# A two-layer mixer and MLP step on one core: side work looked for at every row tile, LRU factors computed inside ScalarE's functions

## The chip, the cores and the metric

The kernel runs on one core of one Trainium2 chip. Its five engines are TensorE (PE in the profile; its weight loads are shown apart as PEld), VectorE (DVE), ScalarE (ACT), GpSimd (POOL) and SyncE (SP), which here only issues transfers. The metric is the device time of one launch in microseconds, lower being better; it is given as the median of several runs.

## The reference, cut to what matters

One inference step of a backbone with two layers. 128 context tokens and 256 latent tokens (384 in all, width 1024, float32) go through each layer; the two groups share the weights but have modulation vectors of their own. Each layer is a mixer of four parallel branches and an MLP, each with a norm before and one behind it:

```python
def trunk_layer(x, cond, P, l, ctx):
    sh1, sc1, g1, sh2, sc2, g2 = modulation(cond, P['ada_w'], P['ada_b'])   # silu(cond) @ (1024 x 6144)
    h = rmsnorm(x, P['norm_mix_pre']) * (1.0 + sc1) + sh1
    y, ctx_out = mixer(h, P, l, ctx)
    x = x + g1 * rmsnorm(y, P['norm_mix_post'])
    h = rmsnorm(x, P['norm_ffn_pre']) * (1.0 + sc2) + sh2
    y = jnp.square(jax.nn.relu(h @ P['mlp_w1'])) @ P['mlp_w2']
    return x + g2 * rmsnorm(y, P['norm_ffn_post']), ctx_out
```

The mixer multiplies h by w_in (13 column groups) and computes A, neighbourhood attention (with a bias table of its own); B, differential attention; C, retention in both directions; D, the RG-LRU in both directions. Two parts of it are touched here:

```python
# retention, one direction: decay inside a chunk of 128 tokens
dmat = jnp.where(mask, jnp.exp(jnp.where(mask, rel, 0.0) * lg[:, None, None]), 0.0)
inner = jnp.einsum('bhnd,bhmd->bhnm', qc, kc) * dmat
# RG-LRU, one direction
r = sigmoid(block_diagonal(x, wa) + ba);  i = sigmoid(block_diagonal(x, wx) + bx)
log_a = -LRU_C * r * softplus(-lam)
a = exp(log_a);  u = sqrt(-expm1(2.0 * log_a)) * (i * x)      # then a linear scan over the tokens
yd = hd * gelu(lr_g)
# the branches are merged
y = (sum over branches of sigmoid(gate_k) * (y_k @ w_branch_k)) @ w_out
```

## The kernel before, in words

**The long products.** All weight products are computed from two-part splits: a weight block is loaded as float32 (tile `raw`) and split into a high part `wh` (ScalarE, sometimes VectorE) and a low part `wl` (VectorE), and the activations likewise (`hh`, `hl` for h; `yh`, `yl` for a branch's result). Each product is three products: high by high, high by low, low by high. `triple` (line 898) issues these three for each row tile k of the contraction, into a PSUM tile `mm`, and yields behind every second k. These products form one stream in a fixed order. For a layer's mixer, in counts of single products: up to 696 the groups of branches B and D, 696 to 792 branch B's gate columns, then its merge; 984 to 1176 retention's q and k; 1176 to 1272 branch D's gates; from 1272 its merge with `w_branch`; 1464 to 1728 the groups of branch A; 1728 branch C's gates; 2016 branch A's gates; 2304 to 2448 `w_out`. A whole layer with its MLP has 3540.

**The side work.** Everything else of the mixer (attention scores, retention, LRU gates, transposes, and the modulation of the next norms, tagged `ada`) is written as generators. `later` (line 611) puts one into a queue with the tag of the branch whose result it belongs to (`yA` to `yD`, or `ada`). `poll` (line 634) runs wherever the stream yields: it goes through the active generators and advances those whose needed tiles are ready by the planner's clock, unless VectorE or ScalarE is more than `BACKLOG = 2.25` us ahead of TensorE. `drain_side` (line 650) runs what is left of a tag, ready or not, where the stream comes to that branch's merge (`need_y`, line 1600).

**The planner.** All this happens while the program is built. `Clock` (line 55) keeps a modelled time for each engine; `Engine` (line 137) wraps every engine, works out a cost for each operation in `cost` (line 165), and books it in `note` (line 101). Hence nearly every operation is recorded at one line, L149. So the costs only set the order in which each engine's instructions are written; on the chip each engine works through its own list and waits for its semaphores. In `note` a VectorE operation that reads SBUF is charged 22% more for the time in which GpSimd is booked as busy. The one-column powers (`small<-small,mhalf 128x1`, a reciprocal square root for a norm) cost 0.52 in `cost`.

**Branch D's side work.** `lg_evac` (line 1217) evacuates the gate input of the RG-LRU, queues the `gelu` of a row tile under `yB`, and `lru_tile` (line 1243) under `yD`: block-diagonal gate products (`y<-setB_x,bia`), tanh on ScalarE, a scaling on VectorE (`tmp<-tmp,lp 128x386`, 16 times), exp and tanh, then the scan, and the split into `yh` and `yl`. Its tile of 386 columns holds 384 tokens and two starts.

**Branch C's side work.** `ret_pair` (line 1356) makes a pair of retention's heads: first the decay tiles (128 x 384 for each head: a `tensor_scalar` and a `scalar_tensor_tensor` over all columns on VectorE, the smaller of two multiples, then exp on ScalarE), then scores, products with v (`y<-v,big`), a norm of the result (`small`, a power on GpSimd, `tmp<-y,small`) and transposes by TensorE (`y<-ident,tmp`). Four pairs in each layer.

**The modulation steps** (`ada`, line 812) take a block of `ada_w`, loaded by SyncE into tile `half`, and add it, times the condition, into an accumulator on VectorE: `big<-half,condT,big 128x512`.

**Branch A's bias** is loaded by GpSimd's queue (`bia<-in_na_rpb`) and given its mask on GpSimd (`bia<-bia,cst`).

Of the kernel before, what the change touches and what calls it, by code (L numbers as in the profile page):

```python
# [55 lines left out]
class Clock:  # L56
# [3 lines left out]

    def __init__(self):
        self.eng = dict(PE=0.0, ACT=0.0, DVE=0.0, POOL=0.0, SP=0.0, Q=0.0, DMA=0.0)
        self.read = {}
        self.ready, self.used, self.slots, self.by, self.free_at, self.parts = {}, {}, {}, {}, {}, {}

    def alloc(self, t, tag, bufs):
# [34 lines left out]
    def note(self, eng, cost, outs, ins, dma=0.0):  # L101
        s = self.eng[eng]
        if eng == "DVE" and any(a.space != PSUM for a in ins):
            cost += 0.22 * max(0.0, min(cost, self.eng["POOL"] - s))
        for a in ins:
            s = max(s, self.when(a, eng))
            if a.space == PSUM:

                by, t = self.read.get(a.name, (eng, 0.0))
                if by != eng:  # L110
                    s = max(s, t + self.HOP[by])
        for a in outs:
            s = max(s, self.free_at.get(a.name, 0.0))
        e = s + cost
        self.eng[eng] = e
        if dma:
            q = self.eng["Q"] = max(self.eng["Q"], e) + 0.47
            e = self.eng["DMA"] = max(self.eng["DMA"], q + 1.6) + dma
            e += 0.9
        for a in ins:  # L120
            if a.space == PSUM:
                self.read[a.name] = (eng, e)
            self.used[a.name] = max(self.used.get(a.name, 0.0), e)
        for a in outs:
            for k in self.keys(a):
                self.ready[k] = e
                self.by[k] = "SP" if dma else eng
            self.used[a.name] = max(self.used.get(a.name, 0.0), e)
# [9 lines left out]
class Engine:  # L138
# [26 lines left out]
    def cost(self, name, aps, k, a):  # L165
        if name == "dma_start":
            return dict(SP=0.06, ACT=0.55, POOL=0.63)[self.key]
        n = max(_size(x) for x in aps)
        psum = any(x.space == PSUM for x in aps)
        if self.key == "ACT":  # L170

            table = (AF.Sqrt in a) if a[2:] and a[2] not in (AF.Copy, AF.Square, AF.Identity, AF.Relu) else self.table
            load = 1.29 if self.table is not None and table != self.table else 0.0
            self.table = table
            half = 0.12 if aps[0].shape[0] == 64 else 0.0
            return load + half + (0.05 if psum else 0.094) + n / 1200 + 0.09 * (len(aps) - 2)
        if self.key == "POOL":
            if k.get("op") == ALU.pow:
                return 0.3 + 0.22 * n
            return 0.1 + n / (290 if name == "tensor_copy" else 390)  # L180
        if self.key == "PE":
            n = _size(aps[0])

            cut = tuple(next(x for x in (32, 64, 128) if a.shape[0] <= x) for a in (aps[1], aps[0]))
            if name == "transpose":
                cut = (128, 128)
            place = (aps[1].start_partition(), aps[0].start_partition())
            switch = 0.0 if cut == self.cut else 0.1
            t = 0.107 if name == "transpose" else max(n / 2195, 0.107) if aps[1].dtype == F32R else max(n / 612, 0.22)
            if switch or cut == (128, 128) or place in self.places:  # L190
                self.places = []
            beside = bool(self.places)
            self.cut = cut
            self.places.append(place)
            return switch + (0.014 if beside else t)
        if name == "reciprocal":
            return 0.07 + n / 120
        if name == "tensor_tensor_scan":
            return 0.04 + n / 425
        extra = 0.06 * sum(x.shape[-1] == 1 for x in aps[1:])  # L200
        if name in ("tensor_scalar", "tensor_copy") and not psum:
            return 0.07 + n / 1920 + extra
        return 0.07 + n / 960 + extra
# [17 lines left out]
def hybrid_flow_kernel(ctx: ExitStack, tc: tile.TileContext, I, O):  # L221
# [272 lines left out]

    RUSH = (0.3, 0.0, 0.0)
    BACKLOG = 2.25

    ADA_LOADS = 3
    ADA_BACKLOG = 1.0
# [133 lines left out]

    def poll():
        admit()
        for task in sorted(active, key=lambda t: t["tag"] == "ada"):
            now = clock.eng["PE"]
            if max(clock.eng["DVE"], clock.eng["ACT"]) > now + BACKLOG or clock.free("y", 6, 2) > now or state["held"] > 4:
                return

            if task["tag"] == "ada" and clock.eng["DVE"] > now + ADA_BACKLOG:
                continue
            need = task["need"]
            n = getattr(need, "n", 0)
            if state["held"] + n > 6 or clock.free("y", 6, max(n, 1)) > now:
                continue
            if need() if callable(need) else clock.at(need) <= now:
                advance(task)
# [249 lines left out]
    def triple(p, pairs):  # L898
        n = len(pairs)
        for i, (ah, al, bh, bl) in enumerate(pairs):  # L900
            mm(p, ah, bh, start=i == 0, stop=False)
            mm(p, ah, bl, start=False, stop=False)
            mm(p, al, bh, start=False, stop=i == n - 1)
            if i % 2:
                yield

    def add_proj_cm(l, c0, n, H, evac, pre=None):

# [58 lines left out]
    def add_layer(l):  # L967
# [212 lines left out]


        S["xd"], S["gg"], S["yD"] = [None] * 4, [None] * 4, [None] * 4
        NL = 386

        def atile():
# [19 lines left out]
                    yield  # L1205
            S["xd"][j] = xd

        def gelu(a, gv):
            yield (a,)
            dve.tensor_scalar(a, a, 0.044715, 1.0, op0=ALU.mult, op1=ALU.add)  # L1210
            dve.tensor_mul(a, a, gv)
# [1 line left out]
            act(a, a, AF.Tanh, scale=GELU_C)  # L1213
            yield (a,)
            dve.scalar_tensor_tensor(gv, a, 1.0, gv, op0=ALU.add, op1=ALU.mult)

        def lg_evac(j, p):
            g = ctile("setB_g")
# [2 lines left out]
            a = atile()[:, 0:NTOK]  # L1221
            act(a, p, AF.Square)
            S["gg"][j] = g
            later(gelu(a, gv), "yB")
            later(lru_tile(j), "yD", (7, 0))
            if j == 3:
                later(S["split_yD"](), "yD")
# [13 lines left out]
                    SP.dma_start(dst, I[n][l, 4 * jh:4 * jh + 4].rearrange("(j q) d e -> (q d) j e", q=2))  # L1241

        def lru_tile(j):
            while "kl" not in LP[l] or S["xd"][j] is None:
                yield
            xd = S["xd"][j][:, 0:NL]
            yield (xd, *S["bia"])
# [20 lines left out]
            for d in range(2):  # L1268
# [1 line left out]
                kl = P("kl")[:, d, j:j + 1]  # L1270
                L, u = ths
                yield (L, u)
                dve.tensor_scalar(L, L, kl, kl, op0=ALU.mult, op1=ALU.add)
                dve.scalar_tensor_tensor(u, u, 1.0, xd, op0=ALU.add, op1=ALU.mult)
                a = tmp()[:, 0:NL]
                act(a, L, AF.Exp)
                act(L, L, AF.Tanh)
                sq = tmp()[:, 0:NL]
                act(sq, a, AF.Square)
                yield (sq,)  # L1280
# [75 lines left out]
        def ret_pair(j):  # L1356
# [3 lines left out]
            for hh in range(2):  # L1360
                h = 2 * j + hh
                a = tmp()[:, 0:384]
                rel = cst[:, C_REL:C_REL + 384]
                dve.tensor_scalar(a, rel, P("nlb")[:, h:h + 1], None, op0=ALU.mult)
                dve.scalar_tensor_tensor(a, rel, P("lg")[:, 0, h:h + 1], a, op0=ALU.mult, op1=ALU.min)
                act(a, a, AF.Exp)
                Dm.append(a)
                yield
            qx = []
# [626 lines left out]
```

## Time and profile before

| | us |
|---|---|
| median of 3 runs (1659.6, 1664.07, 1659.7) | 1659.7 |
| the profiled execution | 1663.42 |
| its span | 1661.6 |
| TensorE busy | 1617.7 |
| VectorE busy | 1172.9 |
| ScalarE busy | 720.0 |
| GpSimd busy | 225.8 |

The span is the time from the first to the last instruction of the profiled execution; what lies outside it is start and end, 1.8 us. "Busy" is the time in which an engine has an instruction under way. In a row of a timeline a value in brackets is the idle time of the engine just ahead of the row, and behind the arrow stands what released it. The granted clock is the share of TensorE's full 2.4 GHz that it was given in a stretch.

### The profile page before, as it was taken

How to read it: one execution, taken by the hardware profiler on the slowest of the kernel's cores; microseconds unless marked ns; L12 is line 12 of the kernel's file. 1: busy time of each engine (PE TensorE's matmuls, PEld its weight loads, DVE VectorE, ACT ScalarE, POOL GpSimd, SP SyncE). 2: the span in 40 equal slices, each digit the busy share in tenths (PEclk: the TensorE clock that was granted, in tenths of full speed). 3: DMA queues.
4: the chain of work that ended last, by engine and by line, in shares of the span. 5: the costliest groups of instructions: out<-in, count | busy, mean ns of one | idle time of the engine just before them, and what ended most of it. 6: DMA issues, size and time to landing. Idle time of an engine off the chain costs nothing.

```text
span 1661.6 us, 24134 instructions
## 1 busy us (share of the span) xinstructions
PE 1617.7 (97%) x9274; PEld 1477.6 (89%) x9274; DVE 1172.9 (71%) x2065; ACT 720.0 (43%) x1389; POOL 225.8 (14%) x290
## 2 busy tenths in 40 slices
PE   6999999999999999999999999999999999999998
PEld 4999998988899898888899999998988988888897
DVE  3696778888796647777678766788878766484444
ACT  3245666333442733333452547633344246333333
POOL 3310100342310100000021110023322100000000
PEclk8999999999999999999999999999999999999999
DMA  9433334357544335656453233445763362463332
GB/s 347 152 117 102 102 121 171 130 143 189 158 150 167 126 106 204 223 196 209 135 164 125 85 115 120 141 156 170 175 166 119 136 215 70 142 215 132 130 125 89
DMA packets 181829, 250.80 MB, mean 151 GB/s; under 512 B 22481, under 2 KB 126722, under 8 KB 181714
## 3 DMA queue, kind: packets, MB, share of 16 engines
q1 hardware_dynamic: 167938, 240.61, 42.9%
q0 software_dynamic: 3936, 5.94, 2.9%
q10 hardware_dynamic: 9840, 2.71, 0.7%
q8 instruction: 73, 1.20, 0.3%
q14 instruction: 42, 0.34, 0.1%
HBM read 243.40 MB, written 5.81 MB: 150 GB/s over the span
## 4 chain that ended last, share of the span: by engine, by line
PE 66%; DVE 7%; ACT 2%; DMA 2%; issue 1%; DVEq 0%; POOLq 0%; SPq 0%; ACTq 0%
PE mm L149 39%; PE y L149 28%; DVE wl L149 2%; DVE tmp L149 2%; DVE big L149 1%; DMA raw<-in_w_in 1%; ACT tmp L149 1%; DMA half<-in_ada_w 1%; ACT big L149 1%; DVE small L149 1%; ACT wh L149 0%; DVE wh L149 0%; ACT half L149 0%; DVE acc L149 0%; DVE half L149 0%
## 5 line engine op out<-in xcount | busy, mean ns | idle before, releaser
L149 PE MATMUL mm<-hh,wh 128*128 128x384 f32 x1536 | 528.1, 344 | 3.6 <-DVE acc L149 2.1
L149 DVE TENSOR_TENSOR wl<-raw,wh 128x1024 fp32r<-128x1024 f32 x315 | 396.2, 1259 | 178.7 <-ACT wh L149 171.2
L149 PE MATMUL mm<-hh,wl 128*128 128x384 f32 x1536 | 518.6, 338 | 0.0
L149 PE MATMUL mm<-hl,wh 128*128 128x384 f32 x1536 | 518.5, 338 | 0.0
L149 ACT ACTIVATE wh<-raw 128x1024 fp32r<-128x1024 f32 x252 | 265.0, 1055 | 215.6 <-PE y L149 131.9
L149 PEld LDWEIGHTS mm<-hh,wh 128*128 128x128 f32 x1536 | 289.0, 188 | 20.4 <-issue 10.4
L149 PEld LDWEIGHTS mm<-hl,wh 128*128 128x128 f32 x1536 | 289.3, 188 | 1.3
L149 PEld LDWEIGHTS mm<-hh,wl 128*128 128x128 f32 x1536 | 288.9, 188 | 0.0
L149 DVE SCALAR_TENSOR_TENSOR big<-half,condT,big 128x512 f32<-128x512 f32 x224 | 168.9, 791 | 5.0 <-DMA half<-in_ada_w 5.0
L149 PE MATMUL y<-wh,yh 128*128 128x512 f32 x312 | 123.4, 396 | 0.0
L149 PE MATMUL y<-wh,yl 128*128 128x512 f32 x312 | 123.3, 395 | 0.0
L149 PE MATMUL y<-wl,yh 128*128 128x512 f32 x312 | 123.2, 395 | 0.0
L149 PE MATMUL mm<-yh,wh 128*128 128x384 f32 x256 | 90.3, 353 | 6.4 <-ACT yh L149 2.9
L149 POOL TENSOR_TENSOR small<-small,mhalf 128x1 f32<-128x1 f32 (+2 forms) x40 | 37.0, 926 | 434.0 <-DVE small L149 434.0
L149 ACT ACTIVATE tmp<-mm 128x384 f32<-128x384 f32 x64 | 31.5, 492 | 143.6 <-PE mm L149 143.6
L149 DVE CAST wh<-raw 128x1024 fp32r<-128x1024 f32 x64 | 44.3, 692 | 63.0 <-PE mm L149 55.3
L149 PE MATMUL mm<-yl,wh 128*128 128x384 f32 x256 | 87.3, 341 | 0.1
L149 PE MATMUL mm<-yh,wl 128*128 128x384 f32 x256 | 87.2, 341 | 0.0
L149 PE MATMUL y<-wh,hh 128*128 128x512 f32 (+1 forms) x192 | 75.1, 391 | 0.2 <-DVE hh L149 0.2
L149 PE MATMUL y<-wh,hl 128*128 128x512 f32 (+1 forms) x192 | 73.8, 384 | 0.3 <-DVE hl L149 0.3
L149 PE MATMUL y<-wl,hh 128*128 128x512 f32 (+1 forms) x192 | 73.7, 384 | 0.0
L149 PEld LDWEIGHTS y<-wl,yh 128*128 128x128 f32 x312 | 58.5, 187 | 14.2
(333 smaller groups left out, 2457.9 us busy)
## 6 DMA issues: line engine op xcount, KB each, us to landing
raw<-in_w_in SPq DMA_DIRECT2D x80, 1024.0 KB
raw<-in_mlp_w SPq DMA_DIRECT2D x64, 1024.0 KB
half<-in_ada_w SPq DMA_DIRECT2D x160, 256.0 KB
raw<-in_w_branch SPq DMA_DIRECT2D x16, 1024.0 KB
raw<-in_w_out SPq DMA_DIRECT2D x8, 1024.0 KB
v<-gscr SPq DMA_DIRECT2D x16, 256.0 KB
bia<-in_na_rpb POOLq DMA_DIRECT2D x32, 96.0 KB, 8.4
raw<-in_ada_w SPq DMA_DIRECT2D x4, 512.0 KB
```

The lines of the kernel that those rows point to most:

```text
L149: r = f(*a, **k)
```

## The change

Five edits. (1) `triple` yields behind every k, so that `poll` runs behind every 3 products of such a piece instead of every 6. (2) `poll` goes through the active generators in the order yB, yD, yC, yA, ada, instead of the order in which they were queued with ada last. (3) The gelu of branch D has the tag yD, and an LRU tile waits (in the planning) until its gelu has been made. (4) The scaling of the LRU is taken into ScalarE's exp and tanh, as a scale and a bias for each partition; the decay tiles are made in three column blocks, since left and right of the diagonal block only one of the two multiples counts: VectorE does the middle 128 columns, ScalarE's exp has the factor as its scale in the outer ones and runs three times. (5) In the planner, a one-column power costs 0.46, and VectorE is charged beside GpSimd only for GpSimd operations of more than 64 elements.

```diff
@@ note
-            cost += 0.22 * max(0.0, min(cost, self.eng["POOL"] - s))
+            cost += 0.22 * max(0.0, min(cost, self.wide - s))
@@ 
+        if eng == "POOL" and _size(outs[0]) > 64:
+            self.wide = e
@@ cost
-                return 0.3 + 0.22 * n
+                return 0.46 if n == 1 else 0.3 + 0.22 * n
@@ poll
+    DUE = ("yB", "yD", "yC", "yA", "ada")
...
-        for task in sorted(active, key=lambda t: t["tag"] == "ada"):
+        for task in sorted(active, key=lambda t: DUE.index(t["tag"]) if t["tag"] in DUE else 0):
@@ triple
-            if i % 2:
-                yield
+            yield
@@ gelu, lg_evac, lru_tile
+            S["gelu"].add(j)
...
-            later(gelu(a, gv), "yB")
+            later(gelu(a, gv, j), "yD")
             later(lru_tile(j), "yD", (7, 0))
...
-            while "kl" not in LP[l] or S["xd"][j] is None:
+            while "kl" not in LP[l] or S["xd"][j] is None or j not in S["gelu"]:
                 yield
...
-                dve.tensor_scalar(L, L, kl, kl, op0=ALU.mult, op1=ALU.add)
+                a = tmp()[:, 0:NL]
+                act(a, L, AF.Exp, scale=kl, bias=kl)
+                act(L, L, AF.Tanh, scale=kl, bias=kl)
                 dve.scalar_tensor_tensor(u, u, 1.0, xd, op0=ALU.add, op1=ALU.mult)
-                a = tmp()[:, 0:NL]
-                act(a, L, AF.Exp)
-                act(L, L, AF.Tanh)
@@ ret_pair
-                dve.tensor_scalar(a, rel, P("nlb")[:, h:h + 1], None, op0=ALU.mult)
-                dve.scalar_tensor_tensor(a, rel, P("lg")[:, 0, h:h + 1], a, op0=ALU.mult, op1=ALU.min)
-                act(a, a, AF.Exp)
+                l_, m_, r_ = slice(0, 128), slice(128, 256), slice(256, 384)
+                lf, lb = P("lg")[:, 0, h:h + 1], P("nlb")[:, h:h + 1]
+                dve.tensor_scalar(a[:, m_], rel[:, m_], lb, None, op0=ALU.mult)
+                dve.scalar_tensor_tensor(a[:, m_], rel[:, m_], lf, a[:, m_], op0=ALU.mult, op1=ALU.min)
+                act(a[:, l_], rel[:, l_], AF.Exp, scale=lb)
+                act(a[:, r_], rel[:, r_], AF.Exp, scale=lf)
+                act(a[:, m_], a[:, m_], AF.Exp)
```

The same products stand in the stream as before; what moves is the side work between them. In a layer's count of single products, the four LRU tiles' gate products stood at 792, 912, 1032 and 1170 and now stand at 747, 846, 948 and 1050. The last retention pair's transposes move from 1680 to 1464, the last modulation step from 2154 to 1911, and the last side work of branch A from 2016 to 1926. Between a retention pair's products with v and its transposes there were 36 single products in six of the eight pairs and 42 in two; the four pairs of a layer now have 27, 33, 27 and 42.

ScalarE, in layer 0, at the end of the last LRU tile, before the change (`th<-mm` evacuates the gates of branch D, whose merge comes next; `yh<-setB_g` is the split of a tile of branch D's result):

```order
L149 ACTIVATE tmp<-tmp 128x386 x3
L149 ACTIVATE th<-mm 128x384
L149 ACTIVATE tmp<-tmp 128x386 x3
L149 ACTIVATE th<-mm 128x384
L149 ACT_TABLE_LOAD
L149 ACTIVATE tmp<-tmp 128x386 x2
L149 ACT_TABLE_LOAD
L149 ACTIVATE th<-mm 128x384 x2
L149 ACTIVATE wh<-raw 128x1024
L149 ACTIVATE yh<-setB_g 128x384
```

The same place after the change:

```order
L151 ACTIVATE tmp<-tmp,lp 128x386 x2
L151 ACTIVATE tmp<-tmp 128x386
L151 ACTIVATE setA_k<-mm 128x384
L151 ACTIVATE wh<-raw 128x1024
L151 ACT_TABLE_LOAD
L151 ACTIVATE tmp<-tmp 128x386 x2
L151 ACTIVATE setA_k<-mm 128x384
L151 ACTIVATE wh<-raw 128x1024
L151 ACTIVATE setA_k<-mm 128x384
L151 ACTIVATE wh<-raw 128x1024
L151 ACTIVATE yh<-setB_g 128x384
```

The split of the last tile stood behind four gate evacuations; it now stands between evacuations of retention's k (`setA_k<-mm`), and the gates' come further down. The LRU's exp and tanh now read the factor from tile `lp`.

VectorE, in layer 0, between the two halves of the norm of the first retention pair, before the change (`small` is the norm's sum, the last row applies it):

```order
L149 TENSOR_REDUCE small<-tmp 128x6
L149 TENSOR_SCALAR small<-small 128x6
L149 SCALAR_TENSOR_TENSOR big<-half,condT,big 128x512 x4
L149 TENSOR_TENSOR wl<-raw,wh 128x1024
L149 TENSOR_TENSOR tmp<-y,small 128x384
```

After the change:

```order
L151 TENSOR_REDUCE small<-tmp 128x6
L151 TENSOR_SCALAR small<-small 128x6
L151 SCALAR_TENSOR_TENSOR big<-half,condT,big 128x512 x2
L151 TENSOR_TENSOR wl<-raw,wh 128x1024
L151 TENSOR_TENSOR tmp<-y,small 128x384
```

Two modulation steps stand there instead of four.

GpSimd, in layer 0, around the first loads of branch A's bias, before the change (the powers `128x6` are of retention's pairs):

```order
L149 TENSOR_TENSOR small<-small,mhalf 128x6
L149 DMA bia<-in_na_rpb 64x6x64 x8
L149 TENSOR_TENSOR tmp<-tmp,setA_q 128x256 x2
L149 TENSOR_TENSOR small<-small,mhalf 128x6
L149 TENSOR_TENSOR bia<-bia,cst 128x384 x2
```

After the change:

```order
L151 TENSOR_TENSOR small<-small,mhalf 128x6
L151 TENSOR_TENSOR tmp<-tmp,setA_q 128x256 x2
L151 TENSOR_TENSOR small<-small,mhalf 128x6
L151 TENSOR_TENSOR acc<-acc,th 128x384 x4
L151 DMA bia<-in_na_rpb 64x6x64 x8
L151 DMA half<-in_ada_b 2x512 x2
L151 TENSOR_TENSOR bia<-bia,cst 128x384 x2
```

The power of the last pair stood behind eight of the loads, and now stands ahead of them and of four additions of branch D's merge.

## Rows read from the trace of the kernel before

**Rows 1.** The page: busy time, share of the span and instructions of each engine.
```profile
PE 1617.7 (97%) x9274; PEld 1477.6 (89%) x9274; DVE 1172.9 (71%) x2065; ACT 720.0 (43%) x1389; POOL 225.8 (14%) x290
```
**Rows 2.** Windows: length, then PE, PEld, DVE, ACT, POOL busy, clock, DMA share, GB/s.
```profile
50.00:504.00 454.00, 446.22 (x2721) 418.55 (x2720) 363.08 (x725) 209.65 (x432) 95.90 (x102) 1.00 0.46 140
268.00:340.00 72.00, 68.86 (x407) 65.88 (x407) 63.81 (x108) 28.71 (x49) 20.73 (x16) 0.98 0.46 160
504.00:577.00 73.00, 70.81 (x377) 63.29 (x376) 47.36 (x83) 36.13 (x83) 5.28 (x7) 0.98 0.44 153
842.00:1302.00 460.00, 450.05 (x2764) 421.90 (x2764) 360.90 (x676) 215.34 (x454) 89.90 (x114) 0.99 0.45 139
```
**Rows 3.** Timeline of TensorE: start, us, operation, count, idle before and its releaser.
```profile
265.33 1.57 PE L149 MATMUL y<-setB_x,bia 64*128 64x386 f32 x8
...
289.56 0.44 PE L149 MATMUL mm<-yh,wh 128*128 128x384 f32 x1 [2.87 <-ACT yh L149]
```
**Rows 4.** The chain that ended last, in order of time: start, us, what.
```profile
698.30 8.48 PE mm L149 x48
```
**Rows 5.** Windows after two waits (granted clock third from the end).
```profile
290.90:294.30 3.40, 3.40 (x12) 3.40 (x12) 3.37 (x6) 2.00 (x5) 1.68 (x2) 0.50 0.01 1
1250.00:1257.00 7.00, 6.30 (x21) 5.79 (x20) 5.52 (x15) 4.25 (x13) 4.24 (x5) 0.51 0.55 191
```
**Rows 6.** Waits of TensorE: in total, times, longest.
```profile
PE y L149 <- DVE tmp L149: 3.3, 2, 2.2
```
**Rows 7.** Timeline of VectorE beside the last retention pair, 385 to 391.
```profile
385.40 3.51 DVE L149 SCALAR_TENSOR_TENSOR big<-half,condT,big 128x512 f32<-128x512 f32 x4
388.83 2.02 DVE L149 TENSOR_TENSOR wl<-raw,wh 128x1024 fp32r<-128x1024 f32 x1
```
**Rows 8.** Timeline of GpSimd, the same time.
```profile
387.34 2.42 POOL L149 TENSOR_TENSOR bia<-bia,cst 128x384 f32<-128x384 f32 x2
```
**Rows 9.** Timeline of VectorE, 307 to 312: a retention pair.
```profile
307.34 2.73 DVE L149 SCALAR_TENSOR_TENSOR big<-half,condT,big 128x512 f32<-128x512 f32 x4
...
311.13 0.55 DVE L149 TENSOR_TENSOR tmp<-y,small 128x384 f32<-128x384 f32 x1
```
**Rows 10.** Timeline of VectorE, 1245 to 1249.
```profile
1245.57 2.74 DVE L149 SCALAR_TENSOR_TENSOR big<-half,condT,big 128x512 f32<-128x512 f32 x4 [4.60 <-DMA half<-in_ada_w]
```
**Rows 11.** Timeline of TensorE, 1248 to 1250.
```profile
1248.82 0.44 PE L149 MATMUL mm<-yh,wh 128*128 128x384 f32 x1 [1.87 <-DVE th L149]
```
**Rows 12.** Groups of VectorE by form: busy us, mean ns, idle before.
```profile
L149 DVE TENSOR_SCALAR tmp<-tmp,lp 128x386 f32<-128x386 f32 x16 | 7.6, 477 | 1.6 <-ACT tmp L149 1.6
L149 DVE TENSOR_SCALAR tmp<-cst,nlb 128x384 f32<-128x384 f32 x16 | 7.4, 460 | 0.0
L149 DVE SCALAR_TENSOR_TENSOR tmp<-cst,lp,tmp 128x384 f32<-128x384 f32 x16 | 10.5, 657 | 0.6
L149 DVE SCALAR_TENSOR_TENSOR setB_g<-tmp,setB_g 128x128 f32<-128x128 f32 x8 | 2.3, 292 | 0.3
```
**Rows 13.** Groups of ScalarE by form.
```profile
L149 ACT ACTIVATE tmp<-tmp 128x386 f32<-128x386 f32 x64 | 31.5, 524 | 20.4 <-DVE tmp L149 19.6
L149 ACT ACTIVATE tmp<-y,hb 64x386 f32<-64x386 f32 x32 | 18.5, 580 | 10.4 <-PE y L149 9.9
L149 ACT ACTIVATE big<-y,small 128x128 f32<-128x128 f32 x32 | 11.6, 364 | 12.2 <-DVE small L149 10.6 <-PE mm L149 1.6
```
**Rows 14.** Timeline of TensorE, the same pair.
```profile
304.50 1.45 PE L149 MATMUL y<-v,big 128*128 128x64 f32 x12
...
312.20 0.49 PE L149 MATMUL y<-ident,tmp 128*128 128x128 f32 x3
```
**Rows 15.** Timeline of VectorE, 566 to 568.
```profile
566.18 1.41 DVE L149 SCALAR_TENSOR_TENSOR big<-half,small,big 128x512 f32<-128x512 f32 x2
```
**Rows 16.** Timeline of GpSimd, the same time.
```profile
566.31 1.03 POOL L149 TENSOR_TENSOR small<-small,mhalf 128x1 f32<-128x1 f32 x1 [0.17 <-DVE small L149]
```
**Rows 17.** Group of GpSimd by form: busy us, mean ns, idle before.
```profile
L149 POOL TENSOR_TENSOR small<-small,mhalf 128x1 f32<-128x1 f32 x24 | 14.3, 599 | 225.0 <-DVE small L149 225.0
```

More of the change, by code (lines that the diff above doesn't have):

```diff
@@ L62, in __init__ @@
         self.eng = dict(PE=0.0, ACT=0.0, DVE=0.0, POOL=0.0, SP=0.0, Q=0.0, DMA=0.0)
-        self.read = {}
+        self.read, self.wide = {}, 0.0
         self.ready, self.used, self.slots, self.by, self.free_at, self.parts = {}, {}, {}, {}, {}, {}
@@ L1182, in add_layer @@
         S["xd"], S["gg"], S["yD"] = [None] * 4, [None] * 4, [None] * 4
+        S["gelu"] = set()
         NL = 386
@@ L1206, in conv, with gelu @@
             S["xd"][j] = xd
-        def gelu(a, gv):
+        def gelu(a, gv, j):
             yield (a,)
```

## The prediction

> **What bounds the kernel now.** The page comes first: TensorE is busy 97% of the span, VectorE 71%, ScalarE 43%, GpSimd 14% [rows 1]. The built program has 8684 TensorE instructions before and after, and its side products (attention, retention, LRU gates, transposes) interrupt the long products at 147 places before and 145 after. So the change gives TensorE no work and takes none away: only its idle time, and the time it runs at half clock, can move. The windows say where the idle time is. Of 43.9 us in the span (1661.6 - 1617.7), the mixer of layer 0 (50 to 504) has 454.00 - 446.22 = 7.8 us and that of layer 1 (842 to 1302) 460.00 - 450.05 = 9.9 us; the step from mixer to MLP (504 to 577) has 2.2 us [rows 2]. The change works in the two mixers: 17.7 us of idle time, and what the clock costs behind it. VectorE is the engine to look at there: 363.08 of 454.00 us busy, 80%, and 63.81 of 72.00, 89%, in the stretch of branch D's gates [rows 2].
>
> **Part by part.** The times are those of the profiled execution, 1663.4 us, which lies 3.7 above the median of the runs.
>
> *The due dates and the finer search.* In the old order the four LRU tiles start behind branch B, and the last one's gate products stand at 265.33. When TensorE enters the products of branch D, which need what that tile makes, it waits 2.87 us, until 289.56 [rows 3]. In the changed order the same gate products stand 222 main products ahead of this place instead of 102. A main product (one of a layer's long ones, in the order in which the program issues them) takes 8.48 / 48 = 0.177 us [rows 4], so 222 are 39 us, and the tile took 289.56 - 265.33 = 24.2 us [rows 3]. ScalarE's order says it too: the last yh split stood behind four of branch D's gate evacuations and now stands ahead of the first. I count the wait as gone, and with it the half clock behind it: in 290.90 to 294.30 the granted clock was 0.50 (the 1.2 GHz level) and 12 products took 3.40 us instead of 12 x 0.177 = 2.1 [rows 5]. That is -2.9 - 1.3 = -4.2; nothing gained is the other end.
>
> *The last retention pair.* TensorE waited 3.3 us for it in two places, one in each layer [rows 6]. At the first, four modulation steps on VectorE took 3.51 us and a weight split 2.02, while GpSimd added masks for branch A's bias from 387.34 on [rows 7, 8]; elsewhere four such steps took 2.73 [rows 9]. In the new order the pair is over 72 main products (12.7 us) before the loads of that bias are even issued; before, they stood ahead of it, and GpSimd's order shows both. So -3.3, and 0 if another step meets the masks.
>
> *A stall that may stay.* In layer 1 VectorE stood 4.60 us for a load of modulation weights [rows 10]; branch C's evacuation was queued behind it and TensorE waited 1.87 us [rows 11]. Then the clock was 0.51 and 21 products took 6.30 us of busy time instead of 3.7 [rows 5]: 4.5 us in all. The change moves these steps some 190 products forward but keeps them beside the loads of the bias. Ends 0 and -4.5; I take half, -2.2.
>
> *Less work on VectorE.* The 16 scalings of the LRU go: 16 x 0.477 = 7.6 us. The 32 decay operations shrink from 384 to 128 columns, from 0.460 + 0.657 to about 0.292 each: 16 x 0.533 = 8.5 us [rows 12]. These 16 us are off the path wherever TensorE doesn't wait; its idle share of the mixers is 17.7 / 914 = 2%, which makes -0.3; the ends are 0 and -3. ScalarE gets it: 32 evaluations with pointers, at 0.580 instead of 0.524, 1.8 us, and 16 times three pieces of at most 0.364 for one of about 0.524, 9.1 us [rows 13]. ScalarE is busy 425 of the 914 us [rows 2], so this is covered; without cover it would be 11 us over 914.
>
> *The price of the finer search.* A step that is found earlier also has less time to spare. Between a pair's last products with v, done at 305.95, and its transposes, VectorE ended at 311.68: 5.7 us [rows 9, 14]. The old order puts 36 main products between them in six of the eight pairs, 6.4 us (42 in two), the new one only 27 in four, 4.8 us. The new order also has two modulation steps between the pair's operations on VectorE where there were four, 2.73 / 2 = 1.4 us less, so 4.4 us are needed. It fits with 0.4 us to spare where it was 0.6. If VectorE were not relieved, each of the four would come 1.0 late, 3.8 in all, and the steps of branch A, which also lose 6 to 15 products, would double that: 0 to +8. I take +1.5, nearer to the pair that I could count.
>
> *VectorE fuller.* Work that ran over 1362 main products now runs over 1179 (from the first LRU tile to the last side work of the mixer). The 89% of branch D's stretch times 1362 / 1179, less the 16 of 724 us saved, is 100%. At the limit, not past it: +1, ends 0 and +13 (below).
>
> *The other edits.* The charge for a one-column power changes the order alone: in the steps to the MLP, four normalisation pieces go from ScalarE to VectorE in each layer and 20 transposes stand together. The bound on either side is the idle time there, 2.2 us each [rows 2]; I take 0.
>
> What this charge rests on can be read. Two VectorE steps beside a one-column power took 1.41 us [rows 15, 16], no longer than half of the 2.73 for four [rows 9]; beside the masks they were stretched [rows 7, 8]. The Trainium skill, "SBUF — State Buffer", section "Who interferes with whom", says that a VectorE operation with two inputs in SBUF and a GpSimd operation that reads SBUF exclude each other for the whole instruction. The masks agree with it; of the pair in the rows it was the power that took long (1.03 us), so the trace does not show VectorE held by one. By that rule the planner would now overlook some half microsecond at each power.
>
> Sum: -4.2 - 3.3 - 2.2 - 0.3 + 1.5 + 1.0 = -7.5: 1663.4 becomes 1655.9, and the median 1659.7 becomes 1652.2.
>
> **The rivals.**
> - *The waits only move.* For: TensorE's work is the same, the steps of retention and of branch A stand closer to what they wait for, and the order is made from estimates. Against: where I could count, VectorE's queue got shorter by as much. If the closer steps cost their upper end, 8, and the stall stays, the sum is -4.2 - 3.3 - 0.3 + 8 = 0: 1660.
> - *VectorE becomes the bound from branch D's gates to the end of branch A's side work.* For: 89% busy there, and the planner fills what is free with modulation steps. It decides from 100% on; at 105% over 750 products (1176 to 1926 of a layer), 133 us, TensorE falls 6.6 us behind in each layer, 13 in two: -7.5 - 1 + 13 = +5, 1665. Against: the planner holds side work back when VectorE is ahead, and 16 us of work are gone.
> - *Nearly all waits go.* For: the largest ones all come from side work that was late or met the bias loads. The 17.7 us and the clock's 1.3 + 2.6 make 21.6; two thirds of it is 14: 1645. Against: the modulation loads still meet them.
> - *Powers hold VectorE after all.* Unlikely, since two steps beside one kept their time. If half of the 24 one-column powers [rows 17] held VectorE ahead of a wait, each for the 1.03 of the one in the row [rows 16], that is 12 us on top of the forecast: 1664.
>
> **How the numbers follow.** The forecast (4 to 12 us faster) has 0.40, waits that move 0.24, VectorE as the bound 0.18, nearly all gone 0.16, powers 0.02. The likeliest is 1652.2; its own range is 1648 to 1656. Over all cases I give 1640 to 1665: the low end takes in most of the third rival, the high end the second's price. What a measurement of this kernel tells from no change is 0.3%, 5 us. Faster by more than that: 0.35 of the forecast's 0.40, and the 0.16: 0.51. Within it: 0.05 of the forecast and the 0.24: 0.29. Slower: 0.20.
>
> **What would show it.** Right: at branch D's first products no wait for yh, and full clock behind it; no wait for retention's transposes in either layer; TensorE's idle time over the two mixers about 10 us instead of 17.7. Wrong: idle time of TensorE with VectorE as releaser between branch D's gates and branch A's, VectorE at 95% or more there; many waits of 0.3 to 1 us at transposes; half clock in a new place.

## The result and the profile after

The changed kernel takes 1674.5 us (median of 4 runs, 1673.8 to 1675.2), the kernel before 1660.3: 1.0088 times as long, 95% interval 1.0076 to 1.010. The forecast was 1652.2 with a range of 1640 to 1665; the time is slower, and outside.

The busy line of the changed kernel's page answers to [rows 1]; a value in brackets is the share of the span, 1673.4 us:

```profile
PE 1617.8 (97%) x9274; PEld 1474.4 (88%) x9274; DVE 1162.2 (69%) x2054; ACT 730.5 (44%) x1417; POOL 219.2 (13%) x289
```

TensorE is as busy as before (1617.7). The loss is idle time: 1673.4 - 1617.8 = 55.6 us instead of 43.9. VectorE is busy 10.7 us less. So the work did get less, and the waits got more. What TensorE waited for in the kernel before (the first two lines; compare [rows 6]) and in the changed kernel (in total, times, longest):

```profile
PE mm L149 <- DVE th L149: 3.0, 3, 1.9
PE y L149 <- DVE half L149: 1.1, 2, 0.5
...
PE mm L151 <- DVE th L151: 8.0, 6, 2.2
...
PE y L151 <- DVE half L151: 6.4, 6, 2.4
PE mm L151 <- ACT setA_k L151: 4.7, 2, 4.3
PE y L151 <- DVE tmp L151: 2.8, 2, 1.4
PE mm L151 <- DVE wl L151: 2.2, 2, 1.2
```

The wait for `yh` at branch D's merge [rows 3] is gone, as forecast. Those for `th` (evacuations of a branch's merge) and `half` (the end of a modulation) are larger; those for `setA_k` and `wl` are new. And VectorE waits longer for blocks of modulation weights, before (4.60 of it in [rows 10]) and now:

```profile
DVE big L149 <- DMA half<-in_ada_w: 5.0, 2, 4.6
...
DVE big L151 <- DMA half<-in_ada_w: 20.2, 4, 6.8
```

The windows say where. The columns are those of [rows 2]; the first two lines are the mixers of the two layers, the third is layer 0 from retention to branch A, the fourth branch D's merge in it, the last the four microseconds behind a wait:

```profile
50.00:513.00 463.00, 445.41 (x2675) 415.48 (x2674) 354.25 (x712) 216.52 (x449) 92.08 (x102) 0.99 0.44 134
852.00:1314.00 462.00, 448.90 (x2749) 419.33 (x2748) 354.58 (x670) 217.75 (x463) 87.31 (x113) 0.99 0.45 136
...
271.00:390.00 119.00, 111.05 (x660) 102.01 (x659) 100.14 (x177) 38.10 (x79) 38.63 (x36) 0.97 0.55 165
297.00:351.40 54.40, 49.98 (x323) 46.96 (x321) 49.50 (x94) 15.07 (x33) 22.48 (x19) 0.97 0.43 143
345.90:349.90 4.00, 4.00 (x16) 4.00 (x15) 4.00 (x6) 0.00 (x0) 2.77 (x2) 0.57 0.00 0
```

The idle time of the mixers is 17.6 + 13.1 = 30.7 us, before 17.7 [rows 2]. In the third window TensorE lost 7.95 us; the same window of the kernel before:

```profile
271.00:390.00 119.00, 115.00 (x686) 107.39 (x685) 99.64 (x172) 43.72 (x79) 38.71 (x36) 0.99 0.52 153
```

VectorE is equally busy there, 99.64 and 100.14 of 119 us, 84% both times. But equal time is not equal work, since the two kernels get through different parts of the stream in it; the run hold_mixer below compares the same products. What VectorE does in which order can be read at once. At branch D's merge its timeline shows (start, us, operation, count):

```profile
340.04 2.73 DVE L151 SCALAR_TENSOR_TENSOR big<-half,condT,big 128x512 f32<-128x512 f32 x4
342.69 0.54 DVE L151 TENSOR_REDUCE small<-tmp 128x6 f32<-128x384 f32 x1
343.27 0.17 DVE L151 TENSOR_SCALAR small<-small 128x6 f32<-128x6 f32 x1
343.35 1.41 DVE L151 SCALAR_TENSOR_TENSOR big<-half,condT,big 128x512 f32<-128x512 f32 x2
344.68 0.54 DVE L151 SCALAR_TENSOR_TENSOR th<-th,mm 128x384 f32<-128x384 f32 x1
```

and TensorE's beside it:

```profile
342.75 0.34 PE L151 MATMUL mm<-yh,wl 128*128 128x384 f32 x1
345.28 0.44 PE L151 MATMUL mm<-yh,wh 128*128 128x384 f32 x1 [2.18 <-DVE th L151]
```

Six modulation steps stand in VectorE's list ahead of the evacuation that TensorE needs. TensorE waits 2.18 us and then runs at a granted clock of 0.57 (the fifth window, most of it at the lower level), as behind the waits of before [rows 5].

Further on, VectorE's timeline shows the loads:

```profile
365.10 1.22 DVE L151 TENSOR_TENSOR wl<-raw,wh 128x1024 fp32r<-128x1024 f32 x1 [0.27 <-ACT wh L151]
373.16 4.07 DVE L151 SCALAR_TENSOR_TENSOR big<-half,condT,big 128x512 f32<-128x512 f32 x6 [6.84 <-DMA half<-in_ada_w]
...
386.42 0.69 DVE L151 TENSOR_TENSOR half<-y,half 128x512 f32<-128x512 f32 x1 [2.37 <-DMA half<-in_ada_b]
```

A step stands 6.84 us at the head of the list for its block; the weight split behind it is late too, and TensorE waits for it (`wl`, 1.2 us). At 386.42 the end of the modulation waits for its own load, and TensorE, which has the transposes of it next, waits 2.35.

The third retention pair, one of those with 27 products between, was late by 1.40 us at 326.26 (and by as much in layer 1). Its power on GpSimd stood behind four issues of loads for the end of an earlier modulation, and the first of them waited 4.90 us for VectorE (GpSimd, then VectorE):

```profile
321.61 1.56 POOL L151 DMA_DIRECT2D half<-in_ada_b  x2 [4.90 <-DVE half L151]
323.17 1.07 POOL L151 DMA_DIRECT2D half<-in_norm_mix_post  x2
324.25 1.36 POOL L151 TENSOR_TENSOR small<-small,mhalf 128x6 f32<-128x6 f32 x1
```

```profile
325.65 0.56 DVE L151 TENSOR_TENSOR tmp<-y,small 128x384 f32<-128x384 f32 x1 [1.25 <-POOL small L151]
```

At the start of layer 0 there is one more place. ScalarE's list has an exp of the parameter staging (`zt`) ahead of an evacuation of k; VectorE makes its input late, and TensorE waits 4.27 us for `setA_k`:

```profile
82.30 1.28 ACT L151 ACT_TABLE_LOAD   x1
91.59 0.21 ACT L151 ACTIVATE zt<-zt 128x16 f32<-128x16 f32 x1 [8.01 <-DVE zt L151]
92.75 0.22 ACT L151 ACTIVATE zt<-zt 128x16 f32<-128x16 f32 x1 [0.95 <-DVE zt L151]
92.87 0.47 ACT L151 ACTIVATE setA_k<-mm 128x384 f32<-128x384 f32 x1
```

### The profile page after: what moved, and what is told of

It reads as the page before. It is cut to its first block, busy times and chain, and to the rows that moved or that the text cites. A ratio compares the mean times of both kernels' runs of the same rounds, so it can differ in the third digit from the quotient of the medians.

```text
span 1673.4 us, 24148 instructions
## 1 busy us (share of the span) xinstructions
PE 1617.8 (97%) x9274; PEld 1474.4 (88%) x9274; DVE 1162.2 (69%) x2054; ACT 730.5 (44%) x1417; POOL 219.2 (13%) x289
## 4 chain that ended last, share of the span: by engine, by line
PE 77%; DVE 10%; DMA 5%; ACT 4%; issue 2%; POOL 1%; SPq 0%; DVEq 0%; POOLq 0%; ACTq 0%
PE mm L151 48%; PE y L151 30%; DVE big L151 4%; DVE wl L151 2%; DVE tmp L151 2%; DMA half<-in_ada_w 2%; DMA raw<-in_w_in 1%; ACT tmp L151 1%; ACT wh L151 1%; ACT half L151 1%; DMA wl<-in_ada_w 1%; DVE small L151 1%; DMA hh<-in_ada_w 1%; POOL tmp L151 0%; DMA half<-in_ada_b 0%
## 5 line engine op out<-in xcount | busy, mean ns | idle before, releaser
L151 DVE TENSOR_TENSOR wl<-raw,wh 128x1024 fp32r<-128x1024 f32 x316 | 401.3, 1271 | 171.9 <-ACT wh L151 164.3
L151 DVE SCALAR_TENSOR_TENSOR big<-half,condT,big 128x512 f32<-128x512 f32 x224 | 169.9, 797 | 20.2 <-DMA half<-in_ada_w 20.2
L151 ACT ACTIVATE th<-mm 128x384 f32<-128x384 f32 x64 | 31.3, 489 | 92.1 <-PE mm L151 91.8
```

The costliest lines, as they stand in the source:

```text
L151: r = f(*a, **k)
```

## Experiments

Three theories came out of these rows. **S**: the finer search as such costs the time, since side work is written too close to what it needs. **W**: the work moved to ScalarE lets the planner pull everything ahead. **M**: what costs is the modulation steps, which are wanted by nobody in the mixer but were pulled ahead (the last ones of layer 0 from 2154 to 1911) and now stand ahead of operations that TensorE waits for. Medians in us; the ratio is to the kernel before, run on the same chip.

| run | median | ratio, 95% interval |
|---|---|---|
| undo_fine | 1660.4 | 0.9982 to 1.0011 |
| only_fine | 1665.3 | 1.0020 to 1.0043 |
| undo_work | 1675.9 | 1.0077 to 1.0111 |
| ada_b0 | 1666.1 | 1.0029 to 1.0056 |
| hold_mixer | 1643.7 | 0.9892 to 0.9921 |
| before_hold | 1662.1 | 1.0002 to 1.0021 |
| before_early | 1683.9 | 1.0128 to 1.0158 |
| coarse_hold | 1650.4 | 0.9930 to 0.9964 |
| no_loads | 1661.0 | 0.9992 to 1.0012 |
| short_steps | 1648.9 | 0.9921 to 0.9950 |
| hold_no_work | 1655.3 | 0.9960 to 0.9984 |
| hold_coarse_start | 1643.9 | 0.9890 to 0.9923 |
| undo_charge | 1668.7 | 1.0036 to 1.0066 |
| undo_due | 1665.7 | 1.0020 to 1.0044 |
| undo_gelu | 1668.6 | 1.0035 to 1.0082 |
| hold_no_due | 1648.7 | 0.9903 to 0.9949 |

**undo_fine.** `triple` yields behind every second k again, the rest of the change stays.

> The changed kernel, but the products again yield behind every second row tile. Theory S (the finer search as such costs the time: side work is written so early that the engines, which work in order, meet operands that are late): back to 1656 to 1661 us. Theory W (the work taken off VectorE lets the planner pull everything ahead): stays at 1670 or above. Theory M (the modulation steps, pulled ahead, crowd VectorE's queue and the loads): in this order they end at 1848 and 2106 of layer 0, as before, and at 1668 and 1932 of layer 1, as in the changed kernel, so about half of the loss stays: 1665 to 1669.

1660.4, as S had it: the whole loss goes with the finer search. W falls, and M's figure, 1665 to 1669, was missed.

**only_fine.** The kernel before, with the yield behind every k.

> The kernel before, with the finer search alone. S: 1671 to 1675 us, as the whole change. W: 1659 to 1662. M: the modulation steps end at 1752 and 2007 of layer 0 and 1779 and 2028 of layer 1 (before 1842, 2154 and 1884, 2184; changed 1614, 1911 and 1698, 1995), a third of the way or more: 1664 to 1667.

1665.3, 5 of the 14 us: the figure of M, not of S.

**undo_work.** The changed kernel with edit (4) taken back.

> The changed kernel, with the LRU scaling and the decay tiles back on VectorE. S: no better than the changed kernel, 1672 to 1677 us, since VectorE has 16 us more to do. W: back to 1659 to 1662. M: the modulation steps end at 1722 and 1962 of layer 0, 1806 and 2046 of layer 1, about half of the way back: 1665 to 1669.

1675.9, as S had it: W falls again, and M's forecast, which went by where the steps end alone, failed.

**ada_b0.** One number of the changed kernel:

```diff
-    ADA_BACKLOG = 1.0
+    ADA_BACKLOG = 0.0
```

> The changed kernel, but the planner takes a modulation step only while VectorE's modelled time is no more than 0 us ahead of TensorE's (before 1.0): branch C's and A's side work stays within some 20 products of the changed order, and the modulation steps end at 1770 and 2106 of layer 0, 1854 and 2190 of layer 1, nearly where they stood before the change. S and W: 1670 to 1675 us. M: 1660 to 1665, VectorE's idle time for the loads of the modulation weights back from 20.2 to about 5 us, and TensorE's waits for tile half (6.4 us) and for th (8.0 us) mostly gone.

1666.1, just above M's figures. By the place in the stream layer 0 was 15 us faster than in the changed kernel up to its last product (788.9 against 803.7). But the limit also held back the steps of the MLP, and TensorE stood 12 us for them at the end of layer 0:

```profile
PE mm L151 <- DVE big L151: 12.7, 2, 12.0
```

**hold_mixer.** The lower limit in the mixers alone:

```diff
-            if task["tag"] == "ada" and clock.eng["DVE"] > now + ADA_BACKLOG:
+            if task["tag"] == "ada" and clock.eng["DVE"] > now + (ADA_BACKLOG if task["cap"] == (0, 1) else ADA_MIXER):
```

with `ADA_MIXER = 0.0`; the MLP's modulations have the cap (0, 1).

> The changed kernel, but in the mixers alone the planner takes a modulation step only while VectorE's modelled time is not ahead of TensorE's; in the MLPs up to 1.0 us ahead, as it was. The last mixer modulation steps stand at 2106 of layer 0 and 2190 of layer 1 (changed kernel 1911 and 1995). Theory M (the modulation steps pulled ahead are what costs the time): the two mixers as in the kernel with the limit at 0 everywhere, which gained 14.6 us on the changed kernel by the end of layer 0 and 8.2 in the mixer of layer 1, without its stall at the end of layer 0: 1645 to 1653 us, faster than both kernels. If the finer search costs time in itself: 1660 or above.

1643.7, a little below M's range: 30.8 us faster than the changed kernel, and about 1% faster than the kernel before. The window of the third line above:

```profile
271.00:390.00 119.00, 118.81 (x731) 111.26 (x731) 98.91 (x181) 47.52 (x99) 35.03 (x36) 1.00 0.58 174
```

VectorE is as busy as in both other kernels, 83%, and TensorE has 0.19 us of idle time where it had 7.95, at full clock. But TensorE gets 731 instructions done in this window instead of 660. By the place in the stream it looks otherwise. Here are products 1176 to 1464 of layer 0, first in the changed kernel, then in the held one, and then the modulation steps alone, in the same two stretches:

```profile
271.30:351.40 80.10, 75.69 (x490) 71.64 (x488) 71.39 (x136) 26.80 (x61) 28.05 (x23) 0.98 0.46 153
271.30:343.80 72.50, 72.50 (x480) 70.14 (x479) 61.32 (x122) 28.07 (x60) 21.80 (x21) 1.00 0.46 154
...
271.30:351.40 80.10, 0.00 (x0) 0.00 (x0) 31.06 (x42) 0.98 0.46 153
271.30:343.80 72.50, 0.00 (x0) 0.00 (x0) 21.05 (x28) 1.00 0.46 154
```

Over these products VectorE has 71.39 us of work instead of 61.32, and 42 modulation steps instead of 28 are the whole difference (31.06 and 21.05 us). TensorE is idle for 4.41 us, and in the held kernel not at all. A mixer has 96 of these steps in both kernels. So the changed kernel has hardly more work for VectorE in all (1162.2 and 1157.3 us busy); it has more of it in front of these products.

The hold moves other side work too, since it shares VectorE: the four retention pairs now have 48, 36, 39 and 33 products between v and transposes, instead of 27, 33, 27 and 42. So this run alone doesn't separate the steps from what moved with them; short_steps below does. On the page TensorE's busy time falls too, to 1606.8 of 1641.4 us (on the clock's part in this, see the last section):

```profile
PE 1606.8 (98%) x9274; PEld 1468.3 (89%) x9274; DVE 1157.3 (71%) x2048; ACT 736.3 (45%) x1423; POOL 215.8 (13%) x289
```

**before_hold.** The same edit in the kernel before.

> The kernel before, with that same limit in the mixers (last modulation steps at 2448 of layer 0 and 2388 of layer 1, before 2154 and 2184). If holding the steps back is a gain of its own, whatever the search: about as much faster than before as the held changed kernel, 1645 to 1652 us. If only the changed kernel's places are crowded: 1657 to 1661.

1662.1: no gain. But it isn't a clean test. By the place in the stream it was 6.1 us ahead of the kernel before at 2160 of layer 0 (3.0 of them already at 290, ahead of any held step), and gave it back at 2304, where steps held too long were drained ahead of `w_out`, with a wait of 4.8 us in each layer:

```profile
PE y L149 <- DVE half L149: 10.7, 4, 4.8
```

What holding is worth in the kernel before without that drain was not measured.

**before_early.** The kernel before, with `ADA_MIXER = 2.25`: no part of the change, only steps let in sooner.

> The kernel before, with the modulation steps of the mixers let in up to 2.25 us ahead instead of 1.0; nothing else changed, the search stays at every second row tile. The steps end at 1728 and 1992 of layer 0 and at 1770 and 2004 of layer 1, near the changed kernel's 1614, 1911, 1698 and 1995. M: 1667 to 1676 us without any part of the change, with the wait for tile half and the loads back. If the search is the cause by itself: 1658 to 1663.

1683.9: beyond M's figure. Steps pulled ahead cost 23 us with the search left coarse. The waits for `th` and `tmp` are like those of the changed kernel; the one for `half`, which M expected, did not come back (1.6 us):

```profile
PE mm L149 <- DVE th L149: 10.2, 6, 4.3
...
PE mm L149 <- ACT yh L149: 6.1, 2, 5.8
PE y L149 <- DVE tmp L149: 5.5, 1, 5.5
PE mm L149 <- ACT setB_x L149: 3.3, 1, 3.3
```

**coarse_hold.** hold_mixer with the yield behind every second k.

> The changed kernel with the search at every second row tile again, and the steps of the mixers held as in the held kernels. Beside the held changed kernel this is the finer search alone, with the crowding out of the way. If the finer search has a cost of its own (it lost 4 us at the parameter staging ahead of 700 of layer 0): 3 to 6 us faster than the held changed kernel, 1641 to 1648. If it gains once the steps are held: 3 to 6 us slower than it, 1650 to 1657.

1650.4: with the steps held, the finer search is a gain of 6.7 us. S falls: it costs 14 only where it feeds modulation steps into VectorE's list.

**no_loads.** The changed kernel, its order kept word for word on the four computing engines; in `load()` of the mixers only the first transfer is issued, and the steps read that block (the modulation is not the reference's):

```diff
-                SP.dma_start(b, I["ada_w"][l, k * 128:(k + 1) * 128, c:c + 512])
+                if mixer and keep:
+                    clock.note("SP", SP.cost("dma_start", [b, src], {}, ()), [b], [src], SP.moved("dma_start", [b]))
+                else:
+                    SP.dma_start(b, src)
+                    keep.append(b)
```

> The changed kernel with its order of instructions on TensorE, VectorE, ScalarE and GpSimd unchanged, but without the loads of the modulation weights in the mixers (94 of 160 transfers of 256 KB): all steps of a mixer read the first loaded block, so the modulation is wrong from layer 0's post-norm on. If what hurts in the crowded stretches is the loads (steps that wait for their block at the head of VectorE's queue, weight blocks that come late behind them): nearly as fast as the held kernel, 1644 to 1654 us. If it is VectorE's time: 1668 to 1674. Both in equal parts: about 1660.

1661.0, 13.5 us faster than the changed kernel: the figure for loads and VectorE's time in equal parts. The waits for `wl` and most of those for `half` go; those behind steps stay:

```profile
PE mm L151 <- DVE th L151: 6.1, 5, 2.2
...
PE y L151 <- DVE tmp L151: 2.8, 2, 1.4
...
PE y L151 <- DVE half L151: 1.6, 4, 0.5
```

**short_steps.** The changed kernel in its order and with all loads; in the mixers the steps from the second k on run over 64 columns.

```diff
+                            dve.raw.scalar_tensor_tensor(a[:, w], raw[:, w], c, a[:, w], op0=ALU.mult, op1=ALU.add)
```

> The changed kernel with its order and all its transfers, but the modulation steps of the mixers from the second row block on run over 64 columns instead of 512 (the result is wrong): 168 steps of 0.80 us become about 0.2 us, some 100 us of VectorE's time go. If VectorE's time is what hurts: 1642 to 1652 us. If it is the loads, which are then asked for even sooner: 1664 to 1674, with VectorE's idle time for the modulation weights at 20 us or more.

1648.9, 25.6 us faster. TensorE's waits for `th` (but for one of 0.6 us), `tmp` and `wl` go, and the one for `half` stays; VectorE itself waits longer for blocks than in any other run:

```profile
PE y L151 <- DVE half L151: 6.1, 6, 2.4
...
DVE big L846 <- DMA half<-in_ada_w: 28.6, 14, 7.8
```

So VectorE's standing still for a block is not in itself what TensorE pays for. VectorE's time is the larger part of the 30.8 us and the loads the smaller; 13.5 + 25.6 are more than 30.8, so the two overlap. short_steps also takes time off VectorE that the held kernel still has, so its 25.6 is an upper end.

**hold_no_work.** hold_mixer with edit (4) taken back.

> The held changed kernel (1643.7 us) with the LRU scaling and the decay tiles back on VectorE, that is the 16 us of VectorE's time apart from the crowding. By the prediction's term (these 16 us count where TensorE waits, here 2%): 1644 to 1645. If side work holds up TensorE wherever VectorE is fuller: 1648 to 1656.

1655.3: the 16 us of VectorE's work, with the order that the planner makes for them, are worth 11.6 us, not 0.3. TensorE's new waits stand in branch A:

```profile
PE y L151 <- DVE small L151: 5.1, 4, 2.3
...
PE y L151 <- ACT setB_g L151: 3.1, 2, 1.8
```

**hold_coarse_start.** hold_mixer with the added places closed until the parameter staging has been written.

> The held changed kernel, but the added places for side work are used only once the parameter staging of layer 0 has been written. Between 290 and 1176 of layer 0 the held kernel with the coarse search was 4.8 us ahead of the one with the fine search, where ScalarE's evacuation of k stood behind an exp of the staging for 4 us. If that place is the cause: 1638 to 1641 us, the fastest of all. If the finer search costs as much at whatever stands there: 1643 to 1645.

1643.9 us, the same as hold_mixer: the expectation failed. The wait for `setA_k` was gone, and the profiled execution was 6.4 us ahead of hold_mixer's at 1176 of layer 0 (264.9 against 271.3), but only 2.0 by the end of the layer (786.5 against 788.5), with new waits of 1.0 us at 1365 and 2.5 at 1803: a wait that moved.

**undo_charge, undo_due, undo_gelu.** The changed kernel with one edit taken back: the charges (5), the polling order (2), the tag of the gelu and the wait for it (3).

> The changed kernel with the planner's old charges (0.52 for a one-column power, VectorE charged beside every operation of GpSimd). The modulation steps of layer 0 end some 50 products later (1662 and 1944 instead of 1614 and 1911), those of layer 1 stay. If the lighter charge is what lets the finer search crowd VectorE: 1662 to 1667 us. If it is not: 1671 to 1676.

> The changed kernel with the generators polled in the order in which they were queued, modulation last. The modulation steps end earlier still (1581 and 1839 of layer 0, 1665 and 1923 of layer 1). By the crowding: 1674 to 1682 us. If the due dates are what costs (side work of branch D ahead of branch C's): 1662 to 1668.

> The changed kernel with the gelus tagged with branch B again and LRU tiles that do not wait for them. The modulation steps of layer 1 end 78 and 102 products earlier (1620 and 1893), those of layer 0 where they were. By the crowding: 1674 to 1680 us. If the later gelus are what crowds VectorE behind branch D's gates: 1662 to 1668.

1668.7, 1665.7 and 1668.6: each takes back some 6 to 9 us (for undo_gelu the interval just touches that of the changed kernel). undo_charge lies between its two figures, undo_due inside its second and undo_gelu just above it. So M's expectation failed in undo_due and undo_gelu. In undo_due the steps end earlier than in the changed kernel in both layers, and yet it is 8.7 us faster: how far the steps have moved doesn't set the time by itself; what they stand ahead of does. The three gains and undo_fine's 14.1 make 34.5 us, more than the whole loss of 14, so the loss belongs to no one edit but to the order that they make together. Which pairing of edits makes it was not taken further.

**hold_no_due.** hold_mixer with the old polling order.

> The held changed kernel (1643.7 us) with the old polling order. If due dates gain what the prediction gave them (the wait at branch D's merge, 4.2 us, partly also the work of the finer search): 1645 to 1649 us. If they gain nothing with the steps held: 1642 to 1645.

1648.7, inside the first range. The due dates are worth about 5 us by the medians, but the intervals of the two ratios overlap. The reason given for that range doesn't hold: TensorE waits for no `yh` in this run either. It waits for `th` (1.0 us), `wl` (0.8) and `tmp` (0.5 twice), where hold_mixer has none of these.

## Why the prediction was wrong, point by point

- *The due dates and the finer search (-4.2).* The wait for `yh` went, and the clock was full there (1.00 from 297 to 345). It doesn't hang on both edits: the wait is gone in only_fine, which has the finer search alone, and in undo_fine, which has all but the finer search; before, before_hold and before_early, with neither, have it. One sign was misread: the four gate evacuations were not what held up the split, since ScalarE stood idle ahead of it, waiting for VectorE:

```profile
288.99 0.52 ACT L149 ACTIVATE yh<-setB_g 128x384 fp32r<-128x384 f32 x1 [2.40 <-DVE setB_g L149]
```

  The merge behind it got waits for `th`, 0.83 and 2.18 us in layer 0, which the term didn't count.
- *The last retention pair (-3.3).* It stood clear of the masks, as counted from the order. The third pair took its place: 2.8 us of waits for `tmp` instead of 3.3 [rows 6].
- *A stall that may stay (half of -4.5).* Wrong in sign. VectorE's idle time for modulation blocks went from 5.0 to 20.2 us, and TensorE's waits for `wl` and `half` came with it. That the steps move some 190 products forward was read from the order and then given no price; this is the step that failed. What the runs show in its place: steps let in sooner cost 23 us by themselves (before_early), and held back in the changed kernel they give 30.8 us (hold_mixer), the larger part of it VectorE's time and the smaller the loads.
- *Less work on VectorE (-0.3).* With the steps held it is 11.6 us, beyond the end of -3. Pricing it by TensorE's idle share of 2% was wrong, since the planner writes another order for it. In the changed kernel the same edit brought nothing that can be measured (1.5 us).
- *The price of the finer search (+1.5, up to 8).* In the changed kernel 14.1 us, with the steps held -6.7. The prediction priced the slack of a retention pair, with two modulation steps less inside it, and not the places where those steps went.
- *VectorE fuller (+1, up to 13).* The second rival came nearest, with 1665 and the right side, but its condition, 105% over 750 products, was not met: VectorE was at 84% over the third window and at 91% (49.50 of 54.40 us) in the fourth. The term spread the work evenly over 1179 products, while 42 of the mixer's 96 steps came in 288 of them. For 20 us VectorE was full in the changed kernel, and nearly so at another place in the held one:

```profile
335.30:355.30 20.00, 17.82 (x101) 16.74 (x100) 19.97 (x34) 4.63 (x7) 8.90 (x6) 0.91 0.64 214
...
387.30:407.30 20.00, 19.64 (x132) 17.65 (x132) 19.51 (x45) 10.26 (x34) 6.71 (x8) 1.00 0.69 178
```

  In the first TensorE is idle for 2.18 us, in the second for 0.36. So a full VectorE costs TensorE time when the operation that it needs stands behind steps that nobody needs yet.
- *The other edits (0).* With the charges taken back the changed kernel gains 5.8 us. This shows a price of the order that they make, not that a power holds VectorE. The trace of the kernel before speaks against the last rival: four VectorE steps `setB_g<-raw,setB_x` (128x256, both inputs in SBUF) beside a one-column power took 0.41 to 0.46 us, and 0.42 without one; four `big<-half,small,big` took 0.75, and 0.75 without.

In short: beside the held kernel the changed one loses 30.8 us, because the edits let the modulation steps into places where they hold up VectorE, GpSimd and the loads. With the steps held the changed kernel is 17.1 us faster than the kernel before (1660.8 in that comparison), and three of its parts, taken away one by one, are worth 6.7, 11.6 and about 5 us there. How much of the 17.1 the holding alone would bring stays open, since before_hold lost most of its lead in drains.

## What to carry to other kernels

A finer search and a lighter engine don't only help the work that is late; the planner also spends them on work that nobody waits for. Before forecasting, see which filler moves ahead in the order, and what stands directly behind it on an engine that works in order. An engine's busy share over a stretch of time doesn't tell this: 83% and 84% went with TensorE idle for 0.2 and for 8 us of the same 119. Compare two kernels by the place in the stream: over the same 288 products VectorE had 61 and 71 us to do.

## What was not expected of the hardware

Fewer waits also made TensorE's work shorter, but at no fixed rate. From the changed kernel to hold_mixer TensorE's idle time fell from 55.6 to 34.6 us, and its busy time, for the same 9274 instructions, from 1617.8 to 1606.8: 11 us more, of 32 in all. The mean granted clock rose from 0.991 to 0.995: the share that was not granted, 0.009 of 1673.4 us and 0.005 of 1641.4, shrank by some 7 us. The rest of the 11 is not explained. The kernel before doesn't fit a rule: it had only 43.9 us of idle time, but a clock of 0.988 and the same busy time as the changed kernel. Executions of one kernel differ too: on the chip of the last comparison the kernel before took 1655.6 us at a clock of 0.995 and 1664.0 at 0.989.
